# A diffusion layer's opening: conditioning products with two stationary columns, and the residual copies moved behind the first SwiGLU block

## The chip, the cores and the metric

The kernel runs on one core of one Trainium2 chip. The metric is the device time of one execution in microseconds, lower is better. Three runs of the kernel before took 1798.3, 1798.21 and 1794.08 us: median 1798.21 us. The profile belongs to one more execution.

## The reference, cut to what matters

One layer of a diffusion backbone works on 512 latent tokens `x` and 256 context tokens `ctx`, 1024 channels each, all in float32. The part that the change touches is the conditioning and the first feed-forward block:

```python
mods   = split(silu(c)     @ w_mod + b_mod, 9)      # shift, scale, gate three times over, for the latent
mods_c = split(silu(c_ctx) @ w_mod + b_mod, 9)      # the same for the context
modulate(x, w, shift, scale) = rmsnorm(x, w) * (1 + scale) + shift
swiglu(x, w_in, w_out) = (silu(a) * b) @ w_out      # a, b = split(x @ w_in)
h  = h  + 0.5 * g1  * swiglu(modulate(h,  norm_ffn1, sh1,  sc1),  w_ffn1_in, w_ffn1_out)
hc = hc + 0.5 * g1c * swiglu(modulate(hc, norm_ffn1, sh1c, sc1c), w_ffn1_in, w_ffn1_out)
```

After it come a retention branch and a convolution branch with sigmoid gates, a second feed-forward block and a final RMSNorm. The change leaves them as they are. `w_mod` is 1024 x 9216, so the nine modulation vectors are a product of two rows (c and c_ctx) with a large matrix.

## The kernel before, in words

**Layout.** Channels lie on the 128 partitions, in eight blocks b = 0 to 7; tokens lie along the free dimension. Columns `xs` (0 to 511) are the latent tokens, `cx` (512 to 767) the context's. Large products are done in three TensorE instructions (`mm3`, L113 to L115): each operand is split into a rounded high part and the remainder, and high x high, low x high and high x low are added up in PSUM. A `unit` (L99 to L107) loads a 512 KB weight tile on SP's queue, rounds it on ScalarE (L104) and takes the remainder on VectorE (L106). There are four buffers each for the raw, high and low tiles.

**The opening.** `cs` holds silu(c) and silu(c_ctx) as two columns per block of 128 input channels. `crow` holds them as rows, and L157 spreads each row over all partitions into `ccrow` with a stationary row of ones (one contraction row, 512 columns per instruction; each f32 matmul is two instructions). `ccrow` is used where VectorE, not TensorE, computes a modulation value: as a multiply with a summed result (L198, L212).

`start` (L522 on) loads x, takes the sum of squares per token, and then goes through the eight blocks. For each b it calls `load_mods(b + 1)`, which loads two blocks of `w_mod0` on SP's queue: i = 0 is the scale, i = 1 the shift. The buffers of the scale blocks (`sg` and `wm`) hold four b at a time; the shift blocks have a place each. `first_mods(b)` (L180) then computes the two columns of scale and, for b < PE_SHIFT = 4, of shift on TensorE: eight products of a 128x128 weight block, stationary, with the two columns of `cs`, moving (L186). For the other b, `shift` computes it on VectorE, for the latent's column there and for the context's later. `norm_start(b, ...)` (L511 on) makes the modulated, split input `u[b]`. `products(n, k1)` is a step of the first two SwiGLU units' products, for all b below k1; the units' weights are `w1i[0]`, asked for at b = 0, and `w1i[1]`, asked for at b = 1. The same is then done for the context's columns, with the same weights.

**What sets the order.** One in-order queue per engine. The program gives dependencies and priorities; the order in each queue is laid out from them before the run, so instructions of neighbouring steps stand mixed in a queue. SP's queue issues the weight loads, and a load that has to wait for its buffer holds up all loads behind it. POOL's queue issues the modulation loads of later steps (`mods`, L206) and the additions into DRAM.

**The sums in DRAM.** `hdram` holds the residual stream of the first block. It is filled by two copies from DRAM to DRAM, x (2 MB) and ctx (1 MB), on ScalarE's queue (L448, L449). `part_sum` then adds each group's output product to it by an accumulating DMA from POOL (L610), and `open_h` reads it back.

Of the kernel before, what the change touches and what calls it, by code (L numbers as in the profile page):

```python
# [16 lines left out]
P = 128  # L17
D = 1024
KT = D // P
L = 512  # L20
# [35 lines left out]

PE_SHIFT = 4

# [6 lines left out]
def hybrid_layer_kernel(ctx: ExitStack, tc: tile.TileContext, a: dict, out: bass.AP):  # L65
# [23 lines left out]
    def ps(shape=(P, 512)):  # L89
        count[0] += 1  # L90
        return pp.tile(list(shape), F32, tag="ps", name=f"ps_{count[0]}")
# [44 lines left out]
    crow = [raw_tile((P, D)) for _ in range(2)]  # L136
    for v in range(2):
        nc.scalar.dma_start(crow[v][0:1, :], a["cc"][:, v * D:(v + 1) * D])
    rope = cp.tile([P, 144], F32, name="rope")
# [10 lines left out]
    nc.scalar.activation(cs, cs, AF.Silu)  # L150

    ccps = []
    for v in range(2):
        nc.scalar.activation(crow[v][0:1, :], crow[v][0:1, :], AF.Silu)
        for i in range(2):
            pb, c = ps(), slice(512 * i, 512 * i + 512)
            nc.tensor.matmul(pb, ones[0:1, :], crow[v][0:1, c], start=True, stop=True)  # L157
            ccps.append((ccrow[v][:, c], pb))
# [21 lines left out]
    def first_mods(b):  # L180

        pm = ps()
        for i in range(2 if b < PE_SHIFT else 1):
            raw = shifts[b, i]
            for k in range(KT):
                nc.tensor.matmul(pm[:, 2 * i:2 * i + 2], raw[k // 4][:, k % 4 * P:(k % 4 + 1) * P], cs[:, k, :],  # L186
                                 start=k == 0, stop=k == KT - 1)
        nc.vector.tensor_scalar(ab1[:, 0, b, :], pm[:, 0:2], bm1[:, 8 + b:9 + b], vec[:, V_N1 + b:V_N1 + b + 1],
                                ALU.add, ALU.mult)
        if b < PE_SHIFT:  # L190
            nc.vector.tensor_scalar_add(ab1[:, 1, b, :], pm[:, 2:4], vec[:, V_BM + b:V_BM + b + 1])
        else:
            shift(b, 0)
# [240 lines left out]
    def ffn1(u):  # L434
# [12 lines left out]
        todo_g = start(ux, uc, gate)  # L447
        nc.scalar.dma_start(hdram[:, :, xs], a["xT"])  # L448
        nc.scalar.dma_start(hdram[:, :, cx], a["ctxT"])  # L449
        t = [operands(kb) for kb in range(4)]  # L450
# [71 lines left out]
    def start(u, uc, gate):  # L522
# [17 lines left out]
        for b in range(KT):  # L540
# [7 lines left out]
            norm_start(b, xs, r1, deriv["x1"], *u[b])  # L548
            if b == 1:
                w += units(a["w1i"][1])  # L550
            if b >= 1:
                products(0, b)
            if b >= 3:
                products(1, b - 1)
# [595 lines left out]
```

## Time and profile before

| | us |
|---|---|
| runs: median, lowest, highest | 1798.21, 1794.08, 1798.3 |
| the profiled execution | 1795.23 |
| its span | 1793.5 |
| TensorE matmuls busy | 1746.4 (97% of the span) |
| TensorE weight loads busy (beside the matmuls) | 1529.3 (85%) |
| VectorE busy | 1134.5 (63%) |
| ScalarE busy | 667.0 (37%) |
| POOL busy | 112.3 (6%) |

The span runs from the first to the last recorded instruction. Rows of the order-of-time view begin with the start and the length in microseconds, then engine, line, operation and tiles (`out<-in`), the shape and how many instructions the row merges; brackets give the idle time of the engine before it and what ended that. "1*128" or "128*128" is rows and columns of the stationary operand, the shape behind it that of the moving operand. Matmuls overlap each other, so the distance from start to start, not the length, says how fast a chain of them goes. "PEclk" is the TensorE clock that was granted, as far as it is recorded.

### The profile page before, as it was taken

To read this page: it belongs to the slowest core of one execution; us is meant where nothing else is said; L and a number is where in the kernel's file an instruction comes from. 1 tells how busy PE (TensorE), PEld (TensorE's weight loads), DVE (VectorE), ACT (ScalarE), POOL (GpSimd) and SP (SyncE) were. 2 spreads that over 40 slices of the span, in tenths; PEclk is the share of its full clock that TensorE was granted. 3 is DMA by queue.
4 is the path that set the end of the run, shared out by engine and by line. 5 is a ranking of instruction groups with operands and counts; after the bars stand their busy time and mean duration, and the time that the engine had idled before them with its cause. 6 is when DMAs were issued, how large, how long until landed. Compare 5 with 4: busy or idle time off the path is not lost.

```text
span 1793.5 us, 22479 instructions
## 1 busy us (share of the span) xinstructions
PE 1746.4 (97%) x8974; PEld 1529.3 (85%) x8974; DVE 1134.5 (63%) x1792; ACT 667.0 (37%) x933; POOL 112.3 (6%) x201
## 2 busy tenths in 40 slices
PE   7999999999999789999999999999999999999997
PEld 6888999998989778888888888888888988888887
DVE  3495777796756878884777579383765643333335
ACT  3353444344443532342343333233473332222222
POOL 0002020112121100000000000001010000000000
PEclk9999999999999899999999999999999999999999
DMA  8427373757593421151123114214562233222221
GB/s 306 146 83 181 101 195 100 194 170 212 157 241 112 170 71 67 40 185 61 59 99 134 61 62 162 71 48 161 190 212 94 71 116 96 94 90 99 105 82 48
DMA packets 68958, 221.96 MB, mean 124 GB/s; under 512 B 8115, under 2 KB 10163, under 8 KB 68853
## 3 DMA queue, kind: packets, MB, share of 16 engines
q1 hardware_dynamic: 44928, 146.82, 24.4%
q0 software_dynamic: 21120, 69.50, 14.0%
q10 hardware_dynamic: 2804, 4.21, 0.6%
q8 instruction: 70, 1.15, 0.3%
q14 instruction: 36, 0.29, 0.0%
HBM read 192.18 MB, written 31.46 MB: 125 GB/s over the span
## 4 chain that ended last, share of the span: by engine, by line
PE 87%; DVE 5%; issue 4%; DMA 3%; ACT 1%; POOL 0%; DVEq 0%; ACTq 0%; SPq 0%; POOLq 0%
PE ps L113 24%; PE ps L114 24%; PE ps L115 24%; PE ps L410 10%; PE ps L186 2%; DMA wm<-in_w_mod 1%; DVE h L706 1%; DVE wl L106 1%; PE ps L275 0%; DVE t L212 0%; DMA gc<-hdram 0%; PE ps L262 0%; DMA hx<-in_xT 0%; PE ps L261 0%; DVE t L724 0%
## 5 line engine op out<-in xcount | busy, mean ns | idle before, releaser
L104 ACT CAST wh<-wraw 128x1024 fp32r<-128x1024 f32 (+2 forms) x212 | 219.4, 1037 | 571.2 <-PE ps L114 309.6
L106 DVE TENSOR_TENSOR wl<-wraw,wh 128x1024 fp32r<-128x1024 f32 (+2 forms) x212 | 254.5, 1203 | 194.5 <-ACT wh L104 189.5
L113 PE MATMUL ps<-uh,wh 128*128 128x512 f32 (+1 forms) x924 | 332.1, 364 | 5.6 <-ACT wh L104 3.3
L115 PE MATMUL ps<-uh,wl 128*128 128x512 f32 (+1 forms) x924 | 331.2, 360 | 0.0
L114 PE MATMUL ps<-ul,wh 128*128 128x512 f32 (+1 forms) x832 | 298.9, 361 | 0.0
L114 PE MATMUL ps<-gx,wh 128*128 128x512 f32 (+1 forms) x544 | 204.0, 377 | 0.0
L115 PE MATMUL ps<-gx,wl 128*128 128x512 f32 (+1 forms) x544 | 204.0, 377 | 0.0
L113 PE MATMUL ps<-gx,wh 128*128 128x512 f32 (+1 forms) x544 | 203.7, 377 | 0.2 <-ACT gx L306 0.2
L113 PEld LDWEIGHTS ps<-uh,wh 128*128 128x128 f32 x924 | 176.0, 192 | 32.6 <-ACT wh L104 4.0
L115 PEld LDWEIGHTS ps<-uh,wl 128*128 128x128 f32 x924 | 176.8, 192 | 25.7
L706 DVE SCALAR_TENSOR_TENSOR h<-y,vec,h 128x512 f32<-128x512 f32 x240 | 179.7, 749 | 5.5
L114 PEld LDWEIGHTS ps<-ul,wh 128*128 128x128 f32 x832 | 159.7, 192 | 23.6 <-issue 0.5
L113 PE MATMUL ps<-hx,wh 128*128 128x512 f32 (+1 forms) x364 | 122.8, 339 | 5.0 <-ACT hx L306 3.4
L114 PE MATMUL ps<-hx,wh 128*128 128x512 f32 (+1 forms) x364 | 123.4, 339 | 0.9 <-DVE hx L307 0.9
L115 PE MATMUL ps<-hx,wl 128*128 128x512 f32 (+1 forms) x364 | 122.8, 338 | 0.0
L113 PEld LDWEIGHTS ps<-gx,wh 128*128 128x128 f32 x544 | 102.1, 188 | 19.1 <-ACT gx L306 0.4
L115 PEld LDWEIGHTS ps<-gx,wl 128*128 128x128 f32 x544 | 102.0, 188 | 18.8
L114 PEld LDWEIGHTS ps<-gx,wh 128*128 128x128 f32 x544 | 102.0, 188 | 18.7
L365 DVE TENSOR_TENSOR wl<-wraw,wh 128x1024 fp32r<-128x1024 f32 x54 | 66.0, 1223 | 55.6 <-ACT wh L364 55.5
L410 PE MATMUL ps<-th,wl 128*128 128x384 f32 x288 | 96.2, 334 | 0.0
L410 PE MATMUL ps<-th,wh 128*128 128x384 f32 x288 | 96.2, 334 | 0.0
L410 PE MATMUL ps<-tl,wh 128*128 128x384 f32 x288 | 96.2, 334 | 0.0
(266 smaller groups left out, 3095.7 us busy)
## 6 DMA issues: line engine op xcount, KB each, us to landing
wm<-in_w_mod POOLq DMA_DIRECT2D x56, 512.0 KB, 4.6
wraw<-in_w1i SPq DMA_DIRECT2D x44, 512.0 KB, 6.4
wraw<-in_w2i SPq DMA_DIRECT2D x44, 512.0 KB, 3.6
hdram<-sg POOLq DMA_DIRECT2D x40, 384.0 KB, 7.7
wraw<-in_w1o SPq DMA_DIRECT2D x16, 512.0 KB, 3.5
wraw<-in_w_cv SPq DMA_DIRECT2D x16, 512.0 KB, 3.6
wraw<-in_w_v SPq DMA_DIRECT2D x16, 512.0 KB, 5.5
wraw<-in_w_rg SPq DMA_DIRECT2D x16, 512.0 KB, 3.6
```

The source lines that it names most:

```text
L104: nc.scalar.copy(hi, raw)
L106: nc.vector.tensor_sub(lo, raw, f32(hi))
L113: nc.tensor.matmul(o, w[0], x[0], start=first, stop=False)
L114: nc.tensor.matmul(o, w[0], x[1], start=False, stop=False)
L115: nc.tensor.matmul(o, w[1], x[0], start=False, stop=last)
L186: nc.tensor.matmul(pm[:, 2 * i:2 * i + 2], raw[k // 4][:, k % 4 * P:(k % 4 + 1) * P], cs[:, k, :], start=k == 0, stop=k == KT - 1)
L365: nc.vector.tensor_sub(lo, src, f32(hi))
L410: nc.tensor.matmul(o, w[i][:, ws], x[k][m], start=first and k == n == 0, stop=k == 3 and n == 2, skip_group_check=True)
L706: nc.vector.scalar_tensor_tensor(o, y[:, t:t + L], vec[:, w0 + t:w0 + t + 1], o, ALU.mult, ALU.add)
```

## The change

- PE_SHIFT becomes 3: the shift of block b = 3 is computed on VectorE.
- `crow` tiles are set to zero over all 128 partitions before their first row is loaded. A new tile `first` (ones in its first row, zeros elsewhere) replaces the one-row stationary operand of L157, so that product contracts over 128 rows.
- `first_mods` takes the two columns of `cs` as the stationary operand and streams the 128 columns of a weight block. The result is two rows of up to 256 values in PSUM; ScalarE copies them to SBUF, and one transpose for the scale and one for the shift turn them back into columns in a second PSUM tile.
- The copies into `hdram` go from ScalarE's queue to POOL's. A DMA of two columns (511 and 512) of the first SwiGLU product into the same place is put ahead of them. It overlaps both copies, so both have to wait for it, and it has to wait for that product. The copies overwrite what it writes.
- The loads of `w1i[1]` are asked for at b = 3 in place of b = 1, and its products begin at b = 4 in place of b = 3.

```diff
-PE_SHIFT = 4
+PE_SHIFT = 3
...
     for v in range(2):
+        nc.vector.memset(crow[v], 0.0)
         nc.scalar.dma_start(crow[v][0:1, :], a["cc"][:, v * D:(v + 1) * D])
...
+    first = tmp((P, P))
+    nc.gpsimd.memset(first, 0.0)
+    nc.gpsimd.memset(first[0:1, :], 1.0)
...
-            nc.tensor.matmul(pb, ones[0:1, :], crow[v][0:1, c], start=True, stop=True)
+            nc.tensor.matmul(pb, first, crow[v][:, c], start=True, stop=True)
...
     def first_mods(b):
+        pm, row, n = ps(), tmp(), 2 if b < PE_SHIFT else 1
+        for i in range(n):
+            c, raw = slice(i * P, (i + 1) * P), shifts[b, i]
+            for k in range(KT):
+                nc.tensor.matmul(pm[0:2, c], cs[:, k, :], raw[k // 4][:, k % 4 * P:(k % 4 + 1) * P],
+                                 start=k == 0, stop=k == KT - 1)
+        nc.scalar.copy(row[0:2, :n * P], pm[0:2, :n * P])
         pm = ps()
-        for i in range(2 if b < PE_SHIFT else 1):
-            raw = shifts[b, i]
-            for k in range(KT):
-                nc.tensor.matmul(pm[:, 2 * i:2 * i + 2], raw[k // 4][:, k % 4 * P:(k % 4 + 1) * P], cs[:, k, :],
-                                 start=k == 0, stop=k == KT - 1)
+        for i in range(n):
+            nc.tensor.transpose(pm[:, 2 * i:2 * i + 2], row[0:2, i * P:(i + 1) * P], ident[0:2, 0:2])
...
         todo_g = start(ux, uc, gate)
-        nc.scalar.dma_start(hdram[:, :, xs], a["xT"])
-        nc.scalar.dma_start(hdram[:, :, cx], a["ctxT"])
+        nc.gpsimd.dma_start(hdram[:, 0, L - 1:L + 1], todo_g[0][:, L - 1:L + 1])
+        nc.gpsimd.dma_start(hdram[:, :, xs], a["xT"])
+        nc.gpsimd.dma_start(hdram[:, :, cx], a["ctxT"])
...
-            if b == 1:
+            if b == 3:
                 w += units(a["w1i"][1])
             if b >= 1:
                 products(0, b)
-            if b >= 3:
+            if b >= 4:
                 products(1, b - 1)
```

## The prediction

> **What bounds the kernel now.** I read the page first, then busy time by stretches of 20 us, then the order of instructions in the opening, then who waited for whom.
>
> ```profile
> span 1793.5 us, 22479 instructions
> PE 1746.4 (97%) x8974; PEld 1529.3 (85%) x8974; DVE 1134.5 (63%) x1792; ACT 667.0 (37%) x933; POOL 112.3 (6%) x201
> ```
>
> TensorE holds the end, and the diff touches only what runs before the second SwiGLU block. So the question is how much sooner TensorE gets through its opening. In stretches (length, then busy time of PE, PEld, DVE, ACT, POOL, then granted clock, DMA share, GB/s):
>
> ```profile
> 0.00:20.00 20.00, 13.40 (x38) 8.70 (x38) 5.32 (x12) 12.93 (x19) 1.87 (x8) 1.00 0.92 331
> 20.00:40.00 20.00, 16.58 (x70) 15.27 (x71) 9.80 (x23) 4.76 (x6) 0.00 (x0) 1.00 0.88 324
> 40.00:60.00 20.00, 20.00 (x82) 18.75 (x83) 7.67 (x21) 4.00 (x6) 0.00 (x0) 1.00 0.79 266
> 60.00:80.00 20.00, 20.00 (x113) 17.29 (x113) 9.14 (x25) 5.99 (x13) 1.09 (x2) 1.00 0.26 92
> 80.00:100.00 20.00, 16.73 (x102) 15.29 (x101) 16.07 (x50) 10.59 (x21) 0.00 (x0) 0.83 0.00 1
> ...
> 20.00:24.00 4.00, 4.00 (x20) 4.00 (x20) 0.00 (x0) 0.00 (x0) 0.00 (x0) 1.00 1.04 410
> 24.00:28.00 4.00, 0.58 (x2) 0.49 (x3) 3.70 (x15) 0.00 (x0) 0.00 (x0) 1.00 0.34 125
> 40.00:44.00 4.00, 4.00 (x20) 4.00 (x21) 0.00 (x0) 0.00 (x0) 0.00 (x0) 1.00 0.27 94
> ```
>
> PE is full from 40 to 80, DMA has holes. But 82 instructions fill the 20 us before 60 and 113 the 20 us after it. The order of instructions (start, length) says why:
>
> ```profile
> 5.07 7.19 PE L157 MATMUL ps<-wraw,ones 1*128 1x512 f32 x8 [5.07 <-ACT wraw L154]
> ...
> 13.79 0.59 PE L261 MATMUL ps<-ones,acc 128*128 128x2 f32 x2 [1.53 <-DVE acc L252]
> ...
> 17.23 3.55 PE L186 MATMUL ps<-cs,sg 128*128 128x2 f32 x16
> ...
> 51.67 3.41 PE L186 MATMUL ps<-cs,sg 128*128 128x2 f32 x16
> ...
> 54.94 0.77 PE L114 MATMUL ps<-ul,wh 128*128 128x512 f32 x1
> 55.51 0.63 PE L115 MATMUL ps<-uh,wl 128*128 128x512 f32 x1
> ...
> 59.35 0.40 PE L114 MATMUL ps<-ul,wh 128*128 128x512 f32 x1
> 65.75 1.84 PE L186 MATMUL ps<-cs,sg 128*128 128x2 f32 x16
> 67.45 0.49 PE L113 MATMUL ps<-uh,wh 128*128 128x512 f32 x1
> ...
> 83.30 0.39 PE L115 MATMUL ps<-uh,wl 128*128 128x512 f32 x1
> 88.97 1.22 PE L113 MATMUL ps<-uh,wh 128*128 128x256 f32 x4 [1.11 <-ACT uh L518]
> ```
> ```profile
> 87.00:88.00 1.00, 0.86 (x2) 0.50 0.00 0
> 92.00:93.00 1.00, 1.00 (x7) 0.50 0.00 0
> 94.00:95.00 1.00, 1.00 (x10) 1.00 0.00 0
> ```
>
> The same sixteen instructions of L186 take 3.41 us at 51.67 and 1.70 at 65.75 (to the next start). The 512-column products go from 0.63 to 0.40 at 59.35. So TensorE runs at half clock up to 59.35, although the column "granted clock" shows 1.00 there: I take that as "no change of clock recorded yet", since the half clock after 87 is recorded as 0.50 with the same slow spacing. Full clock came 4.4 us after dense products began at 54.94, and again some 4.5 us after 88.97. It did not come in 7.19 us of L157 (one row in the array, 512 columns streamed), nor in the 25 us of L186, where each 128-column stationary load serves two streamed columns.
>
> **The change, part by part.** The sum is made against the profiled execution's 1795.23 us; the runs' median, 1798.21, is 3 us above it.
>
> *Stream of scales and shifts.* L186 swaps its operands: the two columns of cs are stationary, 128 columns of weights stream. Its spacing in f32 follows from L275:
>
> ```profile
> 27.61 2.08 PE L275 MATMUL ps<-t,ones 128*128 128x512 f32 x2 [3.42 <-DVE t L268]
> 86.64 1.22 PE L275 MATMUL ps<-t,ones 128*128 128x256 f32 x2 [2.16 <-DVE t L268]
> ```
>
> At half clock 256 columns fewer save 0.86 us in two instructions, so 128 columns cost 0.215 us each: the 0.213 of L186 today. At equal clock a 128x128 block costs the same 3.41 (half) or 1.70 (full). What can change is the clock. Today: twelve blocks (two for b 0 to 3, one for b 4 to 7), nine of them slow, 30.7, and three fast, 5.1: 35.8 us. New: eleven blocks, since PE_SHIFT is 3. I take it that this stream, which fills all 128 rows and moves 128 columns per load, wins the clock as the dense products do, 4.5 us after it begins: 4.5 us slow (1.3 blocks), then 9.7 blocks at 1.70, 16.5: 21.0. **Gain 14.8.** Bounds: no earlier clock, nine slow and two fast, 34.1, gain 1.7; full clock throughout, 18.7, gain 17.1. No row has this shape, so it is the open point. Nearest above are the dense products (all rows, 128 stationary columns: clock won); nearest below L157 (one row: not won). The new stream shares the rows with the first and few columns with neither; I lean to the first: what L157 and today's L186 have in common is that most of the time no column of 128 values is being streamed, and in the new stream one always is.
>
> [...]
>
> *Other slow work in the opening.* Products 54.94 to 59.35, 4.4 us, would be 2.2. L275's 2.08 would be about 1.0, and four early L113 (1.20 for two, below) would save 1.0. **Gain 4.2**; bounds 0 and 4.2.
>
> ```profile
> 36.16 1.20 PE L113 MATMUL ps<-uh,wh 128*128 128x512 f32 x2
> 69.97 0.40 ACT L245 ACTIVATE accc<-hx 128x256 f32<-128x256 f32 x1
> L885 PEld LDWEIGHTS ps<-ident,o 128*128 128x128 f32 x64 | 7.2, 141 | 0.5
> ```
>
> *Copy and transposes.* Eight copies on ACT, up to 256 columns: 0.40 each by L245. ACT is busy 4 to 5 of each 20 us there. Eleven transposes, each one instruction as in L885 (141 ns at full clock, up to twice that at half): 11 x 0.2 = **2.2 lost**. The exposed part is the round trip PE, ACT, PE: about 0.4 plus two handovers, say 0.9 with the transposes' drain. If TensorE has the next block or products queued in between it costs 0, if not 8 x 0.9 = 7. I take the middle, **3.5 lost**: products of finished b are ready beside it, but the queue is strictly what was laid out beforehand. What is late next in the exposed case is norm_start (L517), and with it the products.
>
> *Shift of b = 3 by DVE.*
>
> ```profile
> 68.61 0.69 DVE L198 SCALAR_TENSOR_TENSOR t<-th,kh 128x512 bf16<-128x512 f32 x1
> 59.92 0.27 DVE L200 TENSOR_SCALAR ab<-dots,vec 128x1 f32<-128x1 f32 x1
> 103.80 0.76 DVE L444 TENSOR_TENSOR sg<-sg,ps 128x256 f32<-128x256 f32 x2
> ```
>
> Two L198 and L200 make 1.7 us, once for the latent column and once for the context's. The first falls where DVE is busy 7.67 of 20: hidden under the stream; without that cover 1.7 more. The second joins the stretch where DVE is busy 16.07 of 20 and TensorE follows it: between 0 and 1.7, **1.3 lost**, nearer the upper end as DVE is the fuller of the two.
>
> *first, crow, memsets.* L157 gets 128 rows, same 512 columns, same time; it hides behind the x loads and sums before L261. The memsets of crow (128x1024) go ahead of their loads, and ACT issues those loads and waits for them with its squares queued behind:
>
> ```profile
> 0.83 0.17 DVE L146 MEMSET ones<- 128x128 f32 x1 [0.83 <-PEq L1138]
> ```
>
> Eight times the columns: about 1.0 us each at most. The squares wait for x anyway. Between 0 and 1, **0.5 lost**. L157 might win the clock already; the thin L261 and L262 that follow would lose it again, so I count nothing.
>
> *Copies into hdram.* They leave ACT's queue, go to POOL's, and start only after a two-column write that reads the first SwiGLU product (written by L444, ready at about 104.6 today).
>
> ```profile
> SPq L102 <- DMA hdram<-in_xT: 9.6, 1, 9.6
> SPq L177 <- DMA hdram<-in_ctxT: 8.2, 1, 8.2
> ...
> hdram<-in_xT ACTq DMA_DIRECT2D x1, 2048.0 KB, 15.8
> hdram<-in_ctxT ACTq DMA_DIRECT2D x1, 1024.0 KB, 11.4
> ...
> 126.00 0.53 POOL L206 DMA_DIRECT2D wm<-in_w_mod  x1 [48.44 <-DVE g_c L586]
> 149.97 0.89 POOL L610 DMA_DIRECT2D hdram<-sg  x1 [1.35 <-ACT sg L609]
> ```
>
> SP's queue stood still 17.8 us for them: these are the DMA holes at 24 to 28 and 40 to 44. TensorE did not stand still for it after 28, so by itself this is worth **0**. It is needed once TensorE is faster: x, vec, sixteen 512 KB blocks and four of w1i, 12.8 MB, take 32 us at the 400 GB/s of the full stretches, from about 3 on: the last block lands near 35. With the 3.1 MB of copies it would be 43, with SP's stalls later still. TensorE gets to b = 7 no sooner than about 40, so the floor does not bind; the second w1i pair, moved behind the loads of b = 3 and 4 on SP, lands before products on it begin at b = 4. In the new place: a write, then 16 us, so landed some 25 us after 104.6 today, against 149.97 for the first sum that needs them, both sooner by as much. DMA share at 80 to 100 is 0.00. Queued behind the wait on POOL: rope (needed far later) and perhaps mod loads of L206, of which the next was due at 126. Cost 0; if the cover failed, part sums and the four sg buffers behind them would be late, up to about 10 us.
>
> **Sum:** 14.8 + 4.2 - 2.2 - 3.5 - 1.3 - 0.5 = 11.5 us. 1795.2 - 11.5 = **1784**. With the clock won, the open terms leave about 3.5 each way for the round trips, 1.5 for the context's shift and the start, and 2 more for the moment of the grant on the good side: 1777 to 1789.
>
> **The rivals.**
> - *The clock does not come earlier.* For: two stationary columns use little of the array, f32 streams at half the rate of the products, and L157 failed. Against: L157 had one row. Then 1.7 - 2.2 - 3.5 - 1.3 - 0.5 = -5.8: **1801**, slower. It decides on the spacing of L186 after 22 us: 0.213 instead of 0.106. If the round trips are covered, 1797.5; if all are exposed, 1804.5.
> - *Full clock almost from the start, round trips covered.* L157 wins it and the stream keeps it. Further gains: 2.3 from the first 4.5 us, 1.7 from the sixteen thin pairs of L261 and L262 (13.79 to 17.23, halved), 3.5 round trips, and the 3.4 us before L275 (it waited behind L188 on DVE) filled by the next block: 10.9 more, **1773**.
> - *The clock comes and goes.* The waits for ACT's copies lose it as the gap before 88.97 did. Half of 19.0 is 9.5, less 7.5: **1793**.
> - *The copies do harm in the new place*: part sums wait, up to 10 us: about 1794 with the clock gained.
>
> **How the numbers follow.** Forecast 0.42; late clock 0.32, of which half within 0.3% and half slower; full clock 0.13; comes and goes 0.10; copies harmful 0.03. A measurement of this kernel tells about 0.3%, 5.4 us, from no change. Faster: 0.42 + 0.13 + 0.04 (the better part of the last two) = 0.59. Same: 0.16 + 0.09 = 0.25. Slower: 0.16. The range reaches from the full clock, less 5 for what else it may free, 1768, to most of the late clock, 1803; the forecast's own is 1777 to 1789.
>
> **What would show it.** L186 as 2*128 stationary with 128 streamed columns, spacing 0.213 up to about 22 us and 0.106 after; a recorded grant, or the fast spacing, some 35 us before 59.35. SP without waits on hdram. The end of the first products (L115, today at 83.7) near 71. The copies between about 90 and 115, and the first L610 not waiting for them. The prediction is wrong if L186 keeps 0.213 to its end, if TensorE stands idle in front of each pair of transposes by 1 us or more, or if it waits for w_mod blocks.

## The result, and the profile after

| | before | after |
|---|---|---|
| runs: median, lowest, highest (us) | 1796.64, 1794.08, 1798.3 | 1779.42, 1776.51, 1782.89 |
| span of the profiled execution | 1793.5 | 1779.1 |
| first products end (start of the context's sums, `ones,accc`) | 83.53 | 67.42 |
| first part sum issued (POOL's first accumulating DMA into `hdram`) | 149.97 | 135.56 |

The ratio is 0.9906 [0.9882, 0.993]. In a later comparison, five runs of the changed kernel beside seventeen of the one before gave 1780.85 against 1794.57, 0.9921 [0.9908, 0.9934]: about 14 us. The span shows the same 14.4, and the first part sum comes 14.4 sooner. So the whole gain is made before it.

The page's lines for the kernel after:

```profile
span 1779.1 us, 22499 instructions
PE 1733.1 (97%) x8969; PEld 1506.3 (85%) x8969; DVE 1139.5 (64%) x1803; ACT 669.2 (38%) x941; POOL 115.1 (6%) x206
```

The kernel after from 20 to 80 us in stretches of 20 us (length, then busy time and count of PE, PEld, DVE, ACT, POOL, then granted clock, DMA share, GB/s):

```profile
20.00:40.00 20.00, 19.10 (x127) 12.24 (x124) 9.95 (x24) 7.22 (x12) 0.00 (x0) 0.96 0.76 277
40.00:60.00 20.00, 19.81 (x112) 13.71 (x111) 11.48 (x29) 6.31 (x12) 0.53 (x1) 1.00 0.64 215
60.00:80.00 20.00, 16.72 (x93) 14.51 (x92) 16.34 (x49) 11.84 (x24) 0.54 (x1) 0.91 0.09 27
```

Between 20 and 40 TensorE now does 127 instructions where it did 70. The granted clock in shorter stretches, TensorE alone:

```profile
14.00:15.00 1.00, 1.00 (x10) 0.92 1.00 387
15.00:16.00 1.00, 1.00 (x7) 0.50 1.06 393
...
20.00:21.00 1.00, 1.00 (x7) 0.50 0.99 393
21.00:22.00 1.00, 1.00 (x8) 0.66 1.03 385
```

The clock was lost near 14.85 (0.92 is 0.84 us at full and 0.16 at half) and granted near 21.68. That it could be lost means that it had been won: L161, the old L157 with 128 rows, did that (eight in 6.03 us, where L157 took 7.19). The order of instructions shows the same by their spacing:

```profile
6.67 6.03 PE L161 MATMUL ps<-wraw,t 128*128 128x512 f32 x8 [6.67 <-ACT wraw L158]
13.73 0.38 PE L269 MATMUL ps<-ones,acc 128*128 128x2 f32 x2 [1.03 <-DVE acc L260]
...
16.24 3.57 PE L190 MATMUL ps<-sg,cs 128*2 128x128 f32 x16
19.61 1.91 PE L190 MATMUL ps<-th,cs 128*2 128x128 f32 x8
...
22.98 0.28 PE L195 MATMUL ps<-ident,t 2*128 2x2 f32 x2 [0.45 <-ACT t L192]
23.19 1.12 PE L283 MATMUL ps<-t,ones 128*128 128x512 f32 x2
24.25 1.91 PE L190 MATMUL ps<-sg,cs 128*2 128x128 f32 x16
...
67.19 0.39 PE L115 MATMUL ps<-uh,wl 128*128 128x512 f32 x1
67.42 0.28 PE L269 MATMUL ps<-ones,accc 128*128 128x2 f32 x2
```

Sixteen instructions of L190 take 3.4 us at 16.24 and 1.74 at 24.25 (to the start of what follows). The stream itself wins the clock, 5.4 us after it begins. In stream_only below, where the thin pairs ahead of it still run at the slow spacing (0.43 from pair to pair, against 0.22), its first sixteen instructions take 3.36 us from 17.48 on, the next eight 1.56, and the eight at 22.40 are as fast as those at full clock (a row of 1.04 us): there the clock came within 4.9 us of its start.

Who waited for whom, in the kernel after (engine, line, what it waited for: us in total, times, longest); the first row is TensorE's whole list between 20 and 68 us, the second heads SP's list up to 60, in which `hdram` does not occur:

```profile
PE ps L195 <- ACT t L192: 0.9, 2, 0.5
SPq L176 <- PE ps L190: 8.8, 2, 4.5
```

And POOL's queue in order of time:

```profile
89.29 0.55 POOL L457 DMA_DIRECT2D hdram<-sg  x1 [28.27 <-DVE sg L452]
91.34 0.79 POOL L458 DMA_DIRECT2D hdram<-in_xT  x1 [1.50 <-DMA hdram<-sg]
92.12 0.78 POOL L459 DMA_DIRECT2D hdram<-in_ctxT  x1
...
135.56 0.90 POOL L620 DMA_DIRECT2D hdram<-sg  x1 [1.08 <-ACT sg L619]
```

The copies are issued at 91 and 92 and land in 10.6 and 12.3 us. The first part sum, 43 us behind them, waits for its own `sg` from ScalarE, not for them.

### The profile page after: what moved, and what is told of

Its sections match the earlier page's. It is cut to its first block, busy times and chain, and to the rows that moved or that the text cites. A ratio compares the mean times of both kernels' runs of the same rounds, so it can differ in the third digit from the quotient of the medians.

```text
span 1779.1 us, 22499 instructions
## 1 busy us (share of the span) xinstructions
PE 1733.1 (97%) x8969; PEld 1506.3 (85%) x8969; DVE 1139.5 (64%) x1803; ACT 669.2 (38%) x941; POOL 115.1 (6%) x206
## 3 DMA queue, kind: packets, MB, share of 16 engines
q0 software_dynamic: 21952, 72.64, 14.8%
## 5 line engine op out<-in xcount | busy, mean ns | idle before, releaser
L104 ACT CAST wh<-wraw 128x1024 fp32r<-128x1024 f32 (+2 forms) x212 | 219.4, 1036 | 569.2 <-PE ps L114 323.2
L113 PE MATMUL ps<-uh,wh 128*128 128x512 f32 (+1 forms) x924 | 331.3, 364 | 5.7 <-ACT wh L104 3.4
L115 PE MATMUL ps<-uh,wl 128*128 128x512 f32 (+1 forms) x924 | 330.7, 360 | 0.0
L115 PE MATMUL ps<-gx,wl 128*128 128x512 f32 (+1 forms) x544 | 204.0, 377 | 0.0
L113 PE MATMUL ps<-gx,wh 128*128 128x512 f32 (+1 forms) x544 | 203.7, 378 | 0.2 <-ACT gx L314 0.2
L113 PEld LDWEIGHTS ps<-uh,wh 128*128 128x128 f32 x924 | 174.7, 191 | 34.4 <-ACT wh L104 4.3
L115 PEld LDWEIGHTS ps<-uh,wl 128*128 128x128 f32 x924 | 176.3, 191 | 25.5
L113 PE MATMUL ps<-hx,wh 128*128 128x512 f32 (+1 forms) x364 | 123.1, 340 | 4.5 <-ACT hx L314 2.9
L115 PE MATMUL ps<-hx,wl 128*128 128x512 f32 (+1 forms) x364 | 122.5, 337 | 0.0
L113 PEld LDWEIGHTS ps<-gx,wh 128*128 128x128 f32 x544 | 102.1, 188 | 19.1 <-ACT gx L314 0.4
L115 PEld LDWEIGHTS ps<-gx,wl 128*128 128x128 f32 x544 | 102.0, 188 | 18.7
```

The lines of the kernel that those rows point to most:

```text
L104: nc.scalar.copy(hi, raw)
L113: nc.tensor.matmul(o, w[0], x[0], start=first, stop=False)
L115: nc.tensor.matmul(o, w[1], x[0], start=False, stop=last)
```

## The experiments

All ratios are to the kernel before, run beside the experiment on the same chip, with 95% intervals. "Rest" is the span less the start of the first part sum: what is left once the changed part is over.

| kernel | median, us | ratio | first products end | first part sum | rest |
|---|---|---|---|---|---|
| before | | | 83.53 | 149.97 | 1643.5 |
| after | 1779.42 | 0.9906 [0.9882, 0.993] | 67.42 | 135.56 | 1643.5 |
| stream_undone | 1792.09 | 0.9984 [0.9972, 0.9995] | 75.45 | 142.72 | 1651.6 |
| copies_undone | 1799.84 | 1.0021 [1.0011, 1.0031] | 83.97 | 151.93 | 1644.2 |
| first_undone | 1781.98 | 0.993 [0.9914, 0.9946] | 67.73 | 135.68 | 1642.9 |
| order_undone | 1781.93 | 0.9928 [0.9911, 0.9944] | 68.15 | 135.25 | 1643.7 |
| copies_only | 1796.48 | 1.0016 [1.0005, 1.0027] | 85.28 | 151.74 | 1643.8 |
| stream_only | 1792.84 | 0.9992 [0.998, 1.0003] | 82.97 | 147.45 | 1646.2 |
| copies_back | 1795.55 | 1.0013 [1.0003, 1.0023] | 81.66 | 149.78 | 1643.9 |
| rows_32 | 1799.73 | 1.0029 [1.0018, 1.0041] | 86.15 | 153.72 | 1647.9 |
| casts_pool | 1793.67 | 0.9995 [0.9987, 1.0004] | 79.77 | 147.79 | 1644.1 |
| early_stream | 1783.67 | 0.994 [0.9927, 0.9953] | 65.94 | 133.20 | 1648.9 |
| both_new | 1786.05 | 0.9949 [0.9934, 0.9964] | 69.30 | 137.65 | 1645.1 |
| after_again | 1780.85 | 0.9921 [0.9908, 0.9934] | 65.83 | 134.56 | 1642.9 |

### One part taken out of the kernel after

**stream_undone**: the weight blocks are stationary again, the copies stay on POOL.

```diff
-                nc.tensor.matmul(pm[0:2, c], cs[:, k, :], raw[k // 4][:, k % 4 * P:(k % 4 + 1) * P], ...)
-        nc.scalar.copy(row[0:2, :n * P], pm[0:2, :n * P])
-        pm = ps()
-            nc.tensor.transpose(pm[:, 2 * i:2 * i + 2], row[0:2, i * P:(i + 1) * P], ident[0:2, 0:2])
+                nc.tensor.matmul(pm[:, 2 * i:2 * i + 2], raw[k // 4][:, k % 4 * P:(k % 4 + 1) * P], cs[:, k, :], ...)
```

> The kernel after, with the weight blocks stationary and two moving columns again (no copy, no transposes); the rest of the change stays. Theory 1 (the gain comes from the clock, and the clock is won because full rows of the array are streamed without pause): first wins full clock for L161 and the thin pairs behind it lose it near 15 us; the stream then runs at 0.213 us spacing until dense products begin, first products end near 81 us in place of 67, time 1793 to 1798. Rival (the gain comes from SP's queue no longer standing still for the copies): first products end near 68, time about 1780.

Measured 1792.09: nearly all of the gain is gone in the time. The order of its instructions shows two things:

```profile
16.28 2.01 PE L190 MATMUL ps<-cs,sg 128*128 128x2 f32 x16
...
34.68 3.41 PE L190 MATMUL ps<-cs,wm 128*128 128x2 f32 x16
...
1293.79 1.34 PE L279 MATMUL ps<-t,ones 128*128 128x512 f32 x2 [3.73 <-DVE t L272]
```

The first block still runs for the most part at the clock that L161 won (16 instructions in 1.87 to the next start). But the thin pairs ahead of it and the block itself, all with 128 stationary columns and two streamed ones, do not hold it: 3.27 us for sixteen at 34.68, with a granted clock of 0.50 through the whole stretch from 20 to 40. So here the direction of the stream decided about the clock, and not only the work before it: 0.50 from 20 to 40, against 0.96 after. The first products end 8.0 us later than after. They end 8.1 sooner than before, and sooner than the 81 that was expected: without a shift block at b = 3, and with the second pair asked for later, the dense products begin at 44.77 instead of 54.94 and win the clock near 48.7 instead of 59.35. The copies alone do not do that (copies_only); the other parts were not told apart here. And the first part sum is still 7.3 us sooner than before, while the median gains only 3.1 (ratio 0.9984). The rest of this profiled execution is 8.1 us longer; the last section takes this up.

**copies_undone**: the copies are put back on ScalarE's queue, the rest stays.

```diff
-        nc.gpsimd.dma_start(hdram[:, 0, L - 1:L + 1], todo_g[0][:, L - 1:L + 1])
-        nc.gpsimd.dma_start(hdram[:, :, xs], a["xT"])
-        nc.gpsimd.dma_start(hdram[:, :, cx], a["ctxT"])
+        nc.scalar.dma_start(hdram[:, :, xs], a["xT"])
+        nc.scalar.dma_start(hdram[:, :, cx], a["ctxT"])
```

> The kernel after, with the copies into hdram on ScalarE's queue in the opening again. Theory 1: the stream is fast from 22 us on, but the loads behind SP's two stalls (9.6 and 8.2 us before) come late and TensorE waits for w_mod blocks; first products end 5 to 8 us later, time 1784 to 1788. Rival (the copies were the whole gain): 1795 or more. If the moved copies are worth nothing even now: 1779.

Measured 1799.84, slower than before. But this run doesn't measure the copies alone: the copy of x was laid out in ScalarE's queue ahead of the loads of `crow`, and everything started 9 us late, as one row of TensorE's order shows:

```profile
15.92 6.07 PE L161 MATMUL ps<-wraw,t 128*128 128x512 f32 x8 [15.92 <-ACT wraw L158]
```

copies_back below repeats it with the copy at its old place.

**first_undone**: the product with one row instead of `first`, and no memsets of `crow`.

```diff
-        nc.vector.memset(crow[v], 0.0)
-    first = tmp((P, P))
-    nc.gpsimd.memset(first, 0.0)
-    nc.gpsimd.memset(first[0:1, :], 1.0)
-            nc.tensor.matmul(pb, first, crow[v][:, c], start=True, stop=True)
+            nc.tensor.matmul(pb, ones[0:1, :], crow[v][0:1, c], start=True, stop=True)
```

> The kernel after, with the one-row product of ones for ccrow again (no first, no zeroed crow). Theory 1: the clock that first wins is lost in the thin pairs before the stream begins, so it is worth nothing: time 1778 to 1781, the stream is granted full clock some 3.5 to 7 us after it begins all the same. Rival (first is what wins the clock): the stream stays at 0.213, time 1793 or more.

**order_undone**: PE_SHIFT 4, and the second `w1i` pair asked for and used as before.

```diff
-PE_SHIFT = 3
+PE_SHIFT = 4
-            if b == 3:
+            if b == 1:
                 w += units(a["w1i"][1])
-            if b >= 4:
+            if b >= 3:
                 products(1, b - 1)
```

> The kernel after, with PE_SHIFT 4 and the second w1i pair asked for at b = 1, its products from b = 3, as before. Theory 1: one more block on TensorE, 1.75 us, less 1.7 us of VectorE in the context's stretch; 1779 to 1782. Rival (the order of loads on SP carries part of the gain, because w_mod blocks stand behind the w1i pair): TensorE waits for w_mod, 1783 to 1788.

Both keep the gain: 1781.98 and 1781.93, intervals that overlap that of the kernel after, first part sums within 0.4 us of it. Winning the clock ahead of the stream, and the shift of b = 3, are worth nothing that can be told here. Each was undone alone, not both together.

### One part alone

**copies_only**: the kernel before with the three `hdram` lines of the change and nothing else.

```diff
-        nc.scalar.dma_start(hdram[:, :, xs], a["xT"])
-        nc.scalar.dma_start(hdram[:, :, cx], a["ctxT"])
+        nc.gpsimd.dma_start(hdram[:, 0, L - 1:L + 1], todo_g[0][:, L - 1:L + 1])
+        nc.gpsimd.dma_start(hdram[:, :, xs], a["xT"])
+        nc.gpsimd.dma_start(hdram[:, :, cx], a["ctxT"])
```

> The kernel before with the copies moved to POOL's queue behind the first SwiGLU product, nothing else. Theory 1 (SP's stall is worth nothing while TensorE runs at half clock, full from 29 to 60): first products end near 83.5 us as before, time within 2 us of before, 1793 to 1797. Rival (freeing SP is worth something by itself, as the lost gain of copies_undone hints): first products end near 76, time 1786 to 1789.

**stream_only**: the kernel before with the new `first_mods` and nothing else.

```diff
     def first_mods(b):
+        pm, row, n = ps(), tmp(), 2 if b < PE_SHIFT else 1
...
+                nc.tensor.matmul(pm[0:2, c], cs[:, k, :], raw[k // 4][:, k % 4 * P:(k % 4 + 1) * P], ...)
+        nc.scalar.copy(row[0:2, :n * P], pm[0:2, :n * P])
...
+            nc.tensor.transpose(pm[:, 2 * i:2 * i + 2], row[0:2, i * P:(i + 1) * P], ident[0:2, 0:2])
```

> The kernel before with the new first_mods alone (PE_SHIFT 4, copies in the opening, one-row product for ccrow). Theory 1: the stream wins the clock near 22 us, then TensorE waits for w_mod blocks behind SP's two stalls; first products end between 72 and 78 us, time 1786 to 1791. Rival (without the copies out of the way the stream is worth nothing): first products end near 83, 1793 or more.

The copies alone: 1.0016, if anything 2 to 3 us slower (the first part sum is at 151.74, 1.8 later than before). The stream alone: 0.9992, no difference that can be told. Both together, in first_undone and order_undone with one of the smaller parts left out: 0.993. Neither part is worth anything alone. Where the stream's gain goes is in the waits of stream_only (TensorE, ScalarE and SP's queue, one list each):

```profile
PE ps L191 <- ACT t L188: 11.0, 3, 8.7
ACT wh L104 <- DMA wraw<-in_w1i: 11.3, 2, 11.0
SPq L102 <- DMA hdram<-in_xT: 9.3, 1, 9.3
SPq L177 <- DMA hdram<-in_ctxT: 5.2, 1, 5.2
```

and in its order of instructions, ScalarE and TensorE:

```profile
30.68 1.04 ACT L104 CAST wh<-wraw 128x1024 fp32r<-128x1024 f32 x1 [10.96 <-DMA wraw<-in_w1i]
31.64 0.36 ACT L188 COPY t<-ps 2x256 f32<-2x256 f32 x1
32.14 0.34 PE L191 MATMUL ps<-ident,t 2*128 2x2 f32 x2 [8.70 <-ACT t L188]
```

It is one chain. SP's queue stands still 9.3 us for the copy of x, just where it has to issue the second pair's load (L102). The load is late. ScalarE meets the cast of that load (L104) in its queue and stands 11 us. The row copy (L188), whose input has long been there, is behind it. TensorE needs the row for its transposes and stands 8.7 us, and loses the clock as well: the next sixteen instructions of L186, at 34.41, take 2.61 us, where those at 41.02 take 1.91.

Why SP waits for a copy that ScalarE issued is in the trace too, which records with each DMA the semaphore that counts its landing. SP's and ScalarE's DMAs take turns with the same eight semaphores (107, 109, 110 and 112 to 116 in before and in stream_only), and in both SP stands ahead of a load until the DMA before it with the same semaphore has landed. In before the copy of x, issued at 10.60 with 109, lands 15.8 us later, and SP's next load with 109 is issued at 26.54. In stream_only the copy of x, issued at 10.53, has 109 and lands at 26.84. The eighth load behind it on SP's queue has 109 as well, so SP stands from 17.50 to 26.85. POOL's DMAs have eight semaphores of their own (99 to 106): in the kernel after the copies have 104 and 105, and neither there nor in copies_only does a load of SP wait for them.

**copies_back**: first_undone with the copies on ScalarE again, which here are issued at the old place.

```diff
-        nc.gpsimd.dma_start(hdram[:, 0, L - 1:L + 1], todo_g[0][:, L - 1:L + 1])
-        nc.gpsimd.dma_start(hdram[:, :, xs], a["xT"])
-        nc.gpsimd.dma_start(hdram[:, :, cx], a["ctxT"])
+        nc.scalar.dma_start(hdram[:, :, xs], a["xT"])
+        nc.scalar.dma_start(hdram[:, :, cx], a["ctxT"])
```

> The kernel after with the copies on ScalarE's queue and the one-row product for ccrow, so that the first copy starts near 10.6 us as in the kernel before and not ahead of the cc loads (copies_undone started it at 1.2). Theory 1: some 7 us of the gain are lost to late w_mod blocks, 1785 to 1789. Rival (place of the copy does not matter, the copies cost all of the gain): 1794 or more.

Measured 1795.55, 13.6 us above first_undone, which ran beside other runs of the kernel before; by the two ratios (1.0013 and 0.993) it is some 15. That is the whole gain, as the rival had it, and not the 7 us that were expected. Its waits:

```profile
PE ps L191 <- ACT t L188: 12.7, 2, 12.2
ACT wh L104 <- DMA wraw<-in_w1i: 13.7, 1, 13.7
SPq L172 <- DMA hdram<-in_xT: 9.7, 1, 9.7
```

The same chain in the changed kernel: the stall on SP is 9.7, and TensorE's wait at the end of it is 12.2. Its first products end 13.9 us later than those of first_undone.

**rows_32**: the kernel after, with the stream contracting over 32 rows. It loads the same weights; what it leaves out is three quarters of each sum.

```diff
-                nc.tensor.matmul(pm[0:2, c], cs[:, k, :], raw[k // 4][:, k % 4 * P:(k % 4 + 1) * P], ...)
+                nc.tensor.matmul(pm[0:2, c], cs[0:32, k, :], raw[k // 4][0:32, k % 4 * P:(k % 4 + 1) * P], ...)
```

> The kernel after, whose stream of scales and shifts contracts over the first 32 of each block's 128 input channels only (three quarters of those sums are left out); same number of instructions, same 128 streamed columns. If the clock is won by how many rows of the array are fed: the stream stays at 0.213 us spacing until dense products begin, first products end 8 us or more later, 1788 to 1795. If any unbroken stream of more than one row wins it: as the kernel after, 1779 to 1782.

Its stretches of 20 us:

```profile
20.00:40.00 20.00, 19.10 (x76) 10.22 (x75) 6.99 (x15) 4.33 (x7) 0.00 (x0) 0.50 0.58 218
40.00:60.00 20.00, 20.00 (x74) 10.60 (x71) 6.56 (x15) 4.49 (x8) 0.00 (x0) 0.50 0.51 166
```

One block of its stream, in order of time:

```profile
37.94 3.57 PE L190 MATMUL ps<-wm,cs 32*2 32x128 f32 x16
```

TensorE is as busy as after, streams the same 128 columns per instruction against the same two stationary ones, and stays at half clock from 20 to 60, the products between the blocks included. With 128 rows it is at full clock after 5.4. So of the two things that the prediction weighed, two stationary columns did not keep the clock away here (0.96 and 1.00 from 20 to 60 in the kernel after), and 32 rows did (0.50).

### Can the gain be had otherwise, or more of it

**casts_pool**: copies_back with the casts of the second `w1i` pair moved from ScalarE and VectorE to POOL, so that the cast that stood ahead of the row copy is gone from ScalarE's queue.

```diff
-        nc.scalar.copy(hi, raw)
-        nc.vector.tensor_sub(lo, raw, f32(hi))
+            nc.gpsimd.tensor_copy(hi, raw)
+            nc.gpsimd.tensor_sub(lo, raw, f32(hi))
...
-                w += units(a["w1i"][1])
+                w += units(a["w1i"][1], pool=True)
```

> copies_back with the second w1i pair rounded and subtracted on POOL instead of ScalarE and VectorE. There TensorE stood 12.2 us for ScalarE's copy of the rows, and ScalarE 13.7 us for that pair's load in front of it. If the gain is lost through ScalarE's queue: no such wait, TensorE waits only for w_mod blocks that SP issued after 26 us, first products end near 75 in place of 81.7, time 1786 to 1790. If it is lost because the blocks themselves come late: first products end at 80 or later, 1793 or more.

Measured 1793.67: the gain doesn't come back. ScalarE and TensorE in order of time:

```profile
44.12 0.42 ACT L253 ACTIVATE accc<-hx 128x256 f32<-128x256 f32 x1 [13.69 <-DMA hx<-in_ctxT]
44.45 0.34 ACT L192 COPY t<-ps 2x256 f32<-2x256 f32 x1
44.85 0.37 PE L195 MATMUL ps<-ident,t 2*128 2x2 f32 x2 [10.82 <-ACT t L192]
```

The cast is gone, and the next thing that waits for a late load, a square of the context's channels, stands in its place, with the row copy behind it. That the path leads through ScalarE's queue stands; that it is the cast which matters does not. What matters is that a load is late and anything on ScalarE needs it. What would be left of the loss with nothing on ScalarE in the way is not shown, since TensorE's own blocks behind SP's stall are late as well.

**early_stream**: the kernel after, with the sums of squares (L269, L270) put behind the first block of the stream and the broadcast behind the second, so that no thin products stand between L161 and the stream.

```diff
-        dg = rstd_sum(acc, sq, whole)
         load_mods(0)
...
             first_mods(b)
             if b == 0:
+                dg = rstd_sum(acc, sq, whole)
+                continue
+            if b == 1:
                 r1 = rstd_bcast(dg)
+                norm_start(0, xs, r1, deriv["x1"], *u[0])
             norm_start(b, xs, r1, deriv["x1"], *u[b])
```

> The kernel after with the sums of squares (L269, L270) and the broadcast moved behind the first and second block of the stream, so that the stream follows L161 at once. If L161's clock can be held by the stream: no half clock between 15 and 22 us, first products end 2 to 5 us sooner than in the kernel after (62 to 65), time 1775 to 1778. If blocks arrive too late for that or the thin pairs lose the clock all the same: 1779 to 1782.

**both_new**: early_stream, and products that nothing reads in three gaps of the context's norm.

```diff
+    def keep_clock(n):
+        if n:
+            pz = ps()
+            for _ in range(n):
+                nc.tensor.matmul(pz[:, :LC], ident, accc, start=True, stop=True)
...
-        r1c = rstd_bcast(rstd_sum(accc, sqc, wholec))
+        dgc = rstd_sum(accc, sqc, wholec)
+        keep_clock(5)
+        r1c = rstd_bcast(dgc)
+        keep_clock(2)
...
+        keep_clock(6)
```

> early_stream, and dummy matmuls (ident by accc, 256 columns, into a PSUM tile that nothing reads) in three gaps where TensorE waits: before and after the broadcast of the context's norm (5 and 2), and behind the context's products (6). If they hold the clock over the gaps, the half clock at 70 to 76 and 90 to 97 us goes, worth some 3 us each, less up to 1 us where they overrun the gap: 3 to 5 us below early_stream. If they only delay real work: the same or 1 to 2 us slower than early_stream.

**after_again**: the kernel after itself, beside these.

> The kernel after itself, unchanged, beside the others on the same chip: 1779 to 1782 us, first products end near 67.

Neither is better than the kernel after: 0.994 and 0.9949 against 0.9921 beside them. The 1783.67 of early_stream lies above both times that were expected, though its first part sum is sooner than in either execution of the kernel after (133.20 against 135.56 and 134.56); the last section comes back to this. The first block of the stream in after_again, in order of time:

```profile
15.91 1.91 PE L190 MATMUL ps<-sg,cs 128*2 128x128 f32 x16
...
21.58 1.12 PE L283 MATMUL ps<-t,ones 128*128 128x512 f32 x2 [1.28 <-DVE t L276]
```

The same view of early_stream, with one row from far later that the last section uses:

```profile
13.11 1.91 PE L190 MATMUL ps<-sg,cs 128*2 128x128 f32 x16
...
1281.46 2.01 PE L283 MATMUL ps<-t,ones 128*128 128x512 f32 x2 [2.21 <-DVE t L276]
```

The kernel after, in this second profiled execution, kept by itself the clock that L161 had won: its first block is fast, where in the first execution the same code lost it at 14.85. What early_stream was to mend was not always broken, and the first products end at 65.94 there against 65.83. In both_new the gap behind the first products was filled (the stretch from 60 to 80 shows TensorE busy 19.75 and a granted clock of 1.00, against 16.72 and 0.91 after), but its own second block of the stream ran at half clock, and a part of the added products was laid among the context's; the first part sum came at 137.65, later than after.

## Why the prediction was right, and where its working was not

The forecast was 1784, of its own range 1777 to 1789; the medians are 1779.4 and 1780.9. From the order of instructions I summed what TensorE spent from the start of the last thin product before the stream (17.01 before, 15.96 after) to the context's sums, each instruction from its start to the next start, waits apart:

| | before | after | gain | forecast |
|---|---|---|---|---|
| start of this stretch | 17.01 | 15.96 | 1.05 | -0.5 |
| blocks (L186, then L190) | 35.5 | 23.0 | 12.5 | 14.8 |
| products (L113 to L115) and L275, then L283 | 27.4 | 25.9 | 1.5 | 4.2 |
| wait ahead of L275, then L283 | 3.4 | 0 | 3.4 | 0 |
| transposes (L195) | | 1.4 | -1.4 | -2.2 |
| wait for the row copies | | 0.9 | -0.9 | -3.5 |
| first products to first part sum | 66.4 | 68.1 | -1.7 | -1.3 |
| sum | | | 14.4 | 11.5 |

The first products were to end near 71 and end at 67.4. That the sum came within 3 us owes something to luck: 5.4 us of gain counted too much (blocks, products, the shift of b = 3) stand against 8.4 counted too little (the start, the wait ahead of L275, transposes and round trips).

**The stream wins the clock: right, and for the reason given.** The forecast was 4.5 us at half clock, spacing 0.106 afterwards; measured 5.4 and 0.109 (1.74 / 16). The grant came at 21.68, 37.7 us ahead of the 59.35 of before. Eleven blocks took 23.0 instead of 21.0: the first two 6.3 instead of 5.7, the other nine at 1.74 instead of 1.70, 0.4 more, and the rest is time from a block's last instruction to what follows it. rows_32 is the test of the argument: what the prediction took to be common to the two cases without a grant was that no 128 values are being streamed most of the time. A stream of 32 values at the same rate stayed at half clock. A busy TensorE alone did not bring the grant: rows_32 has it busy 19.10 and 20.00 of 20 us at a granted clock of 0.50, and L157 streamed for 7.19 us in the kernel before without one.

**Round trips: mis-sized, 0.9 instead of 3.5.** TensorE waited twice, 0.45 each, at b = 0 and 1, before there were products to lay between. From b = 2 on none was exposed.

**Other slow work: mis-sized, 1.5 instead of 4.2.** The products before 59.35 were slow and are fast now, but between blocks and transposes some of the new ones are spaced wider than the 0.23 of a run of them (0.34 from the first to the second behind a pair of transposes, at 28.56).

**The wait ahead of L275: put in the wrong place.** The prediction had it go only in the rival with full clock. It went in the forecast's own case, and not because a block was laid into it. VectorE in the kernel before, in order of time:

```profile
24.23 0.28 DVE L188 TENSOR_SCALAR ab<-ps,bm,vec 128x2 f32<-128x2 f32 x1 [10.50 <-PE ps L186]
...
24.55 0.15 DVE L287 TENSOR_SCALAR t<-ps 128x4 f32<-128x4 f32 x1
...
26.69 0.87 DVE L268 TENSOR_SCALAR t<-ident_h,t 128x128 f32<-128x128 f32 x4
```

And in the kernel after:

```profile
17.62 0.16 DVE L295 TENSOR_SCALAR t<-ps 128x4 f32<-128x4 f32 x1 [1.32 <-ACT t L294]
...
19.77 0.87 DVE L276 TENSOR_SCALAR t<-ident_h,t 128x128 f32<-128x128 f32 x4
23.30 0.28 DVE L196 TENSOR_SCALAR ab<-ps,bm,vec 128x2 f32<-128x2 f32 x1 [2.66 <-PE ps L195]
```

The norm's chain (L295 to L276) used to stand behind the first modulation value (L188), which waited 10.5 us for TensorE. As that value now comes later, by way of the row and the transposes, the chain is laid ahead of it and runs while the stream does.

**The copies: the step that failed.** The prediction said that moving them is worth 0 by itself, which copies_only bears out (1.0016), and that it is needed once TensorE is faster because the last blocks would land near 43 with them. Needed it is, but by another way and for far more: 13.6 us, the whole gain. The limit is not the transfers' total. SP stalls for a semaphore that it shares with the copy, and the stall reaches TensorE through ScalarE's in-order queue. In the kernel before the stream's blocks needed nothing from ScalarE, and between 17 and 60 us TensorE has no wait for it, so a late load there cost nothing; the row copy of the change is what ties TensorE to ScalarE's queue. The row that shows the danger is in the profile of before, and the prediction didn't read it:

```profile
30.46 1.04 ACT L104 CAST wh<-wraw 128x1024 fp32r<-128x1024 f32 x1 [10.92 <-DMA wraw<-in_w1i]
```

ScalarE stood 10.9 us for a load that SP's stall had delayed, and the change puts eight instructions of TensorE's path into that queue. The prediction costed them by ScalarE's busy share, 4 to 5 of 20 us, which says nothing of what they queue behind. As the change takes the cause away, this error did not reach the sum.

In the new place the copies harmed nothing, as predicted: issued at 91, landed by 105, needed at 135.6.

**Memsets and `first`:** 0.5 lost was forecast. L161 starts 1.6 later than L157 did (6.67 against 5.07), yet the sums of squares start at the same time (13.73 against 13.79), since they wait for VectorE. first_undone measures nothing either way.

**The shift of b = 3:** 1.7 against 1.3. order_undone, which has it back on TensorE, shows 67.1 us from the first products' end to the part sum, against 68.1 and 68.7 for the kernel after in its two executions. The sign agrees; the size is no better known than by about 1 us.

**The rivals.** "The clock does not come earlier" gave 1801: rows_32, which makes that case, ran 1799.73 (1.0029). "Full clock almost from the start" gave 1773; after_again's profiled execution had its condition, a stream at full clock from 15.91, and took 1779.27. More than half of the 10.9 that this rival added (round trips covered but for 0.9, and the 3.4 ahead of L275) was already in the other execution, and the faster stream then met VectorE: 1.28 us ahead of L283. "The clock comes and goes" gave 1793; here the clock holds from 21.68 to 72.9. With the copies back it does go: behind the wait of 12.2 us the granted clock is 0.50 from 32.5 to 46.2.

## What to carry to other kernels

When a step newly takes something from another engine, price what that engine's queue holds ahead of it, and whose late loads those instructions wait for; its busy share says nothing of that. An edit that is worth nothing by itself can be the condition of another's whole gain, so two parts need four kernels before either is called useless. A long transfer can hold up a queue that did not issue it (here SP's, 9.3 to 10.2 us for ScalarE's 2 MB), so look which semaphore its landing counts and who else waits for that one. And a matrix-vector product with few columns can be turned round so that the wide operand streams: here it had TensorE's full clock 5.4 us after its start with 128 rows, and not once from 20 to 60 us with 32.

## What the runs showed of the hardware that was not expected

**With two stationary columns the clock came when the stream fed 128 rows, and not when it fed 32.** 128 rows: full clock in 5.4 us (after). The same with 32 rows: 0.50 through the 40 us from 20 to 60 (rows_32). 128 stationary columns with two streamed: a clock already won was lost (stream_undone, 0.50 from 20 to 40). Where between 32 and 128 rows the change lies wasn't tried.

**The 2 MB copy from DRAM to DRAM, issued from ScalarE, held up SP's queue**, by the semaphores that the two queues share in this program: SP waits 9.3 to 10.2 us for the 2 MB in the five kernels that have the copies there, and 5.2 to 8.2 for the 1 MB in three of them (before, stream_only, copies_undone). That it is not the traffic as such shows in copies_back, where SP's load waits from 16.09 to 25.86 for semaphore 109, the copy's: the list of its waits puts 9.7 us down to the copy. Issued from POOL the copies count other semaphores (104 and 105), and in the kernel after no load of SP waits for them. Whether POOL's copies would slow the loads in the busy opening was not tried.

**The clock changes recorded in before and after lie whole steps of 3.41 us apart, and in the second execution of the kernel after the steps fell elsewhere.** The clock was lost at 14.85 and granted at 21.68: 6.83 apart, twice 3.41. All changes that the traces of before and after record, 14 and 16, are like that: within each of the two, every one lies whole steps of 3.41 us from every other. Counted in such steps from the span's start, 1.19 us are left over in the first execution of the kernel after. In the second the spacing of the products goes from 0.21 to 0.12 near 75.4, which leaves 0.3 over. The same code lost the clock in the first and kept it in the second (the first block, 3.4 us or 1.7). That the place of the steps decided this is my reading; no run set it.

The rests in the table go from 1642.9 to 1651.6 though the program behind the first part sum is the same, and the clock has a part in that. A good part of the difference arises where TensorE waits for VectorE at the broadcast of the second norm, near 1280 to 1300. In four of the five executions with the longest rests that wait is 1.86 to 3.73 us, with half clock around its end: 3.4 us of it in stream_undone (0.64 and 0.50 in the two stretches of 2 us from 1294 on) and in early_stream and both_new (0.83 from 1280 to 1290), and in stream_only a broadcast of 2.08 us. In rows_32, the fifth, the broadcast takes 1.12. In before, after, after_again and first_undone the wait is 0.51 to 1.36, and the broadcast takes 1.12 or 1.13. There the kernel before shows

```profile
1294.31 1.12 PE L275 MATMUL ps<-t,ones 128*128 128x512 f32 x2 [0.51 <-DVE t L268]
```

0.51 us of waiting and full speed behind it. stream_undone (its row above) waits 3.73 there; early_stream waits 2.21, and its broadcast takes 2.01 instead of 1.12, at half clock. The wait itself does not come from the clock: VectorE's chain for the broadcast stands behind an addition that waits for a transfer of `ypart`. In before and in stream_undone:

```profile
1290.67 1.23 DVE L963 TENSOR_TENSOR wraw<-wraw,wraw 128x1024 f32<-128x1024 f32 x1 [2.51 <-DMA wraw<-ypart]
1290.15 1.23 DVE L969 TENSOR_TENSOR wraw<-wraw,wraw 128x1024 f32<-128x1024 f32 x1 [2.83 <-DMA wraw<-ypart]
```

In before it starts 2.75 us ahead of TensorE's last product before the broadcast (1293.42), in stream_undone 0.48 behind it (1289.67). Why the transfer comes later there, measured by TensorE's progress, stays open. Some is lost around 580 to 610 too, where TensorE waits for ScalarE and VectorE several times and the clock is granted for a larger or smaller part of it: over three stretches of 10 us, from 440 us behind the first part sum on, the mean granted clock is 0.83, 0.97 and 0.69 in first_undone, and 0.59, 0.84 and 0.54 in stream_undone. The order of TensorE's last 8,000 instructions is the same in early_stream as in the kernel after, so it isn't another order. How much of the rest the place of the steps decides was not tested by a run of its own. If they fall anew in each execution, as in the two of the kernel after, it cannot be all of it: over several executions that would even out. But the median of twelve executions of stream_undone gains 3.1 us where its first part sum is 7.3 sooner, and the median of six of early_stream lies 2.8 above that of five of the kernel after beside it, with a first part sum 1.4 sooner (the part sums are of one profiled execution each). What the steady part is stays open. For readers of such results all this means that of a gain in the opening some microseconds can be lost or found a thousand microseconds later, with nothing changed there.
